# A streaming encoder step on one core: the first closing weight's halves pinned among the last gate projections, and the output weight's last halves moved into the first output pair

## The chip, the cores and the metric

The program runs on one core of a Trainium2 chip. The metric is the device time of one execution in microseconds (us), lower being better. TensorE (PE in the profile) does matrix products and transposes; its weight load is listed apart as PEld. VectorE (DVE), ScalarE (ACT) and GpSimd (POOL) do the elementwise work, and transfers are issued from the queues of SyncE (SP) and POOL.

## The reference

The layer normalises its rows, projects them to `q, k, v`, three gate inputs and a pooling input, runs two token mixers, and merges them:

```python
z = rmsnorm(x, norm_g) @ w_in                  # q k v ga u gb mg, 1024 columns each (mg 2048)
att = stick_breaking(q, k, v)                  # 8 heads x 128, causal
pb = multi_scale_pool(u, ...) * pool_scale     # trailing means, per-group linear map
y_a = (att * silu(ga)) @ w_br_a
y_b = (pb * silu(gb)) @ w_br_b
gate = sigmoid(mg)
m = gate[..., :1024] * y_a + gate[..., 1024:] * y_b
y = rmsnorm(x + m @ w_out, final_g)
```

There are 2048 prompt rows and 64 sample rows (the latter with a cache of 4096 positions), all in float32.

## The kernel before

**Number format.** Every float32 operand is used as two fp32r tiles, `hi` (a copy rounded by ScalarE, line 81) and `lo` (the rest, a subtraction on VectorE, line 82). A product of two operands is three matmuls: hi by hi, hi by lo, lo by hi. Making both tiles of an operand is called its split below; `split` is the helper at lines 76 to 82.

**Stages.** The projections, the attention and the pooling of the two row halves come first and take some three quarters of the program. The last piece of that part, called the gate stretch here, projects 15 column slabs of 128 of the merge gate for the second half of the rows (`merge_gate(1, 1)` to `merge_gate(1, 15)`). A slab has two groups of 512 rows, and a group is 24 matmuls into one of two PSUM buffers `pj` (lines 284 to 286). ScalarE then takes the sigmoid of the group (`sgm`, line 302), which frees the PSUM buffer, and SP stores it to DRAM (line 306). The slab's weights come as two loads of 256 KB (`raw`, line 272, three buffers) and are split into `whi` and `wlo` (two buffers), a slab ahead.

**What runs beside the gate stretch.** `run` interleaves the slabs with the generator `before_closing` (from line 955), in steps set by an estimate of TensorE time. It has 21 steps: four and four for the weight sums of `w_br_a` and `w_br_b`, four for the first row forms, and nine for the first forms of `w_br_a`. The closing multiplies 1024 x 1024 weights as 2 x 2 blocks with seven block products instead of eight, so it needs, beside the blocks `b11, b21, b22`, four differences of blocks `t1` to `t4`. `weight_sums` makes these on POOL: loads (line 904), subtractions (906) and stores to the DRAM tensor `tw_d` (907). `forms` reads blocks and differences back in halves of 512 KB (`wraw`, two buffers, line 934), and splits each half. The call in `before_closing` is for `b11, b21, t1, t2` of `w_br_a`: eight halves, the last four of them read from `tw_d`.

**What sets the order.** In this first part the kernel fixes the order on TensorE only. On the other engines and on SP, a scheduler that works from its own estimates of durations orders the instructions within each engine. From the closing on, the order on TensorE, VectorE, ScalarE and SP is the order of the code; POOL keeps the scheduler's.

**The closing.** For `w_br_a` and then `w_br_b`, three row blocks of 704 rows pass through seven products `p` = 0 to 6, so `order` has 42 entries `s`, each with two column halves `cc`. `emit` multiplies a finished block with its gate and writes it (for `w_br_b`, after adding the first branch, `mp`); it also issues the loads of the gates and of `mp` two and three blocks ahead. The counter h = 2s + cc drives `weights_at(h)`, which runs the next step of `forms`: a table `when` says at which h. A step splits one half and issues the load of the half after next into the buffer that comes free.

**The output pairs.** The last stage multiplies the merged rows by `w_out` in eight pairs of 128 rows, again with seven products of 12 matmuls each, in this order: `x = a11 b11`, `z = a12 b21`, `x += s2 t2`, `y = s1 t1`, `x += s3 t3`, `y += s4 b22`, `x += a22 t4`. Between them ScalarE copies partial sums out (`kept`, line 998), VectorE adds them to the residual rows (`join`, lines 1250 and 1251), and the operands of later products are split: `out_b` makes s1 to s4, `out_c` splits s3 and s4, `out_d` splits a22, `out_a` the next pair's a11 and a12. The merged rows of a pair lie in two tiles `mt` and `mb` with one buffer each, so `fetch(n + 1)` can load `mb` only when the split of a22 has read the old one. The halves of `w_out`'s last blocks, `b22` and `t4`, are split at h = 83, 84, 85 and 87 in the kernel before: the first at the end of the last entry of the closing, the second just ahead of the first pair, the third behind the first `kept` of pair 0, and the fourth behind the third.

Of the kernel before, what the change touches and what calls it, by code (L numbers as in the profile page):

```python
# [8 lines left out]
F32 = mybir.dt.float32  # L9
F32R = mybir.dt.float32r  # L10
AF = mybir.ActivationFunctionType
ALU = mybir.AluOpType
# [3 lines left out]
P = 128  # L16
# [28 lines left out]
def kernel(  # L45
# [6 lines left out]
    nc = tc.nc  # L52
# [92 lines left out]
    with ExitStack() as front:  # L145
# [777 lines left out]
                    nc.gpsimd.dma_start(tw_d[i, j, k * P:(k + 1) * P, :], out)  # L923
            return compute

        def form_half(i, nm, k):

            if nm[0] == "t":
                src = tw_d[i, int(nm[1]) - 1]
            else:  # L930
                r, c = (int(x) - 1 for x in nm[1:])
                src = weights[i][r * 512:(r + 1) * 512, c * 512:(c + 1) * 512]
            raw = wright.tile([P, 2, 512], F32, name="wraw", bufs=2)
            nc.sync.dma_start(raw, src[k * P:(k + 2) * P].rearrange("(k p) c -> p k c", p=P))

            def halves():
                if k == 0:
                    wf[i, nm] = [wpool[nm].tile([P, 4, 512], F32R, name=f"{nm}{part}") for part in ("hi", "lo")]
                hi, lo = wf[i, nm]
                split(hi[:, k:k + 2], lo[:, k:k + 2], raw)  # L940
            return halves

        def forms(i, nms):

            todo = [(nm, k) for nm in nms for k in (0, 2)]
            ahead = [form_half(i, *h) for h in todo[:2]]
            yield 1.0
            for n in range(len(todo)):
                ahead.pop(0)()
                if n + 2 < len(todo):  # L950
                    ahead.append(form_half(i, *todo[n + 2]))
                yield 1.0

        def row_form():
# [4 lines left out]
        def before_closing():  # L959
            yield from weight_sums(0)  # L960
            yield from weight_sums(1)
            for p in range(2):
                hi, lo = rf[p] = row_form()
                for k in (0, 2):
                    raw = wright.tile([P, 2, 512], F32, name="wraw", bufs=2)
                    src = aT_d[p * 512 + k * P:p * 512 + (k + 2) * P, 0:NR].rearrange("(k p) r -> p k r", p=P)
                    nc.sync.dma_start(raw[:, :, 0:NR], src)
                    split(hi[:, k:k + 2], lo[:, k:k + 2], raw[:, :, 0:NR])
                    yield 1.0
            yield from forms(0, ("b11", "b21", "t1", "t2"))  # L970
# [21 lines left out]
    ahead = {}  # L992
# [58 lines left out]
    def out_c(n):  # L1051
        group(n, ("s3", "s4"), s34.pop(n))
# [6 lines left out]
    with tc.manual_schedule(engines={E.PE, E.DVE, E.Activation, E.SP}):  # L1059
# [79 lines left out]
        when = {}  # L1139
        for i, base, nms, at in ((0, 2, WFORMS[4:], [5, 6, 7, 8, 9, 10]),  # L1140
                                 (1, 28, WFORMS, [30 + (8 * h) // 5 for h in range(14)]),
                                 (2, 70, WFORMS, [71 + h for h in range(10)] + [83, 84, 85, 87])):
            when.setdefault(base, []).append((i, nms))
            for h in at:
                when.setdefault(h, []).append(None)
# [21 lines left out]
        for s, (i, t, p) in enumerate(order):  # L1167
            r = rf.pop(s)
            more = s - p + 7 < len(order)
            for cc in range(2):  # L1170
                if p == 0:
                    xs_[cc] = bpsum.tile([P, 2, 512], F32, name="x")
                elif p in (1, 3):
                    ys_[cc] = bpsum.tile([P, 2, 512], F32, name="y")
                acc = (xs_ if p in (0, 2, 4, 6) else ys_)[cc]
                for j in range(2):
                    c = 2 * cc + j
                    product(acc[:, j, 0:NR], wf[i, WFORMS[p]], r, p in (0, 1, 3),
                            slice(c * P, (c + 1) * P), slice(0, NR))
                out = acc[:, :, 0:NR]  # L1180
                if p == 0:
                    x1[cc] = kept(out, "x1")
                elif p == 1:
                    emit(out, x1[cc])
                elif p == 2:
                    x2[cc] = kept(out, "x2")
                elif p == 3:
                    x5[cc] = kept(out, "x5")
                elif p == 4:
                    emit(out, x5[cc])  # L1190
                elif p == 5:
                    emit(out, x2[cc])
                else:
                    emit(out, None)
                if cc == 1:
                    make(s + 2)
                    if p == 0:
                        sum4()
                    if more and p == 5:
                        sum3()  # L1200
                    if more and p == 6:
                        sum12()
                if not more and (p, cc) == (4, 1):
                    rowx.close()
                    pool = ctx.enter_context(tc.tile_pool(name="back", bufs=1, side="left"))
                    fetch(0)
                weights_at(2 * s + cc)
                if more and (p, cc) in ((2, 0), (3, 0), (5, 0), (5, 1)):
                    load_rows(s + 7 - p, {2: "r11", 3: "r21", 5: ("r12", "r22")[cc]}[p])
                if not more and (p, cc) == (6, 0):  # L1210
                    xts = residuals(0)


# [39 lines left out]
        def accumulator(nm):  # L1253
            return bpsum.tile([P, 2, 512], F32, name=nm)[:, 0]

        weights_at(84)
        for n, (_, r) in enumerate(pairs):
            wo = {nm: wf.get((2, nm)) for nm in WFORMS}
            f = {nm: of.pop((n, nm)) for nm in ("a11", "a12", "s2", "s1")}
            last = n + 1 == len(pairs)  # L1260
            x = accumulator("x")
            product(x, f["a11"], wo["b11"], True, cols, whole)
            x1 = kept(x, "x1")
            if n:
                norm_sums(1)
            else:
                weights_at(85)
            z = accumulator("y")
            product(z, f["a12"], wo["b21"], True, cols, whole)
            join(xts[0], left, z, x1)  # L1270
            if n:
                norm_root()
            out_c(n)
            f.update((nm, of.pop((n, nm))) for nm in ("s3", "s4"))
            if not last:
                fetch(n + 1)
            else:
                tail = [pool.tile([P, 4, 256], F32, name=nm) for nm in ("mt", "mb")]
                for h in range(2):
                    src = m_d[h * 512:(h + 1) * 512, 1024:RA].rearrange("(k p) r -> p k r", p=P)  # L1280
                    nc.sync.dma_start(tail[h][:, :, 0:DEC], src)
            product(x, f["s2"], wo["t2"], False, cols, whole)
            x2 = kept(x, "x2")
            if n:
                norm_scale()
            y = accumulator("y")
            product(y, f["s1"], wo["t1"], True, cols, whole)
            x5 = kept(y, "x5")
            if n == 0:
                weights_at(87)  # L1290
                out_d(0)
                wo["t4"] = wf[2, "t4"]
                acc = [pool.tile([P, 2], F32, name=f"acc{i}") for i in range(5)]
                for b in range(2):
                    t = gates.tile([P, 2, NR], F32, name="fg_bc", tag="sg", bufs=5)
                    g_bc.append(t.rearrange("p a b -> p (a b)")[:, 0:512])
                    nc.sync.dma_start(g_bc[b], final_g.rearrange("(a d) -> a d", a=1)[:, b * 512:(b + 1) * 512].broadcast_to([P, 512]))
            if not last:
                out_a(n + 1)
            else:  # L1300
# [75 lines left out]
```

## Time and profile before

| What | Value |
|---|---|
| Time, median of 3 runs | 2799.86 us (2798.79 to 2799.97) |
| Time of the profiled execution | 2798.5 us |
| Its span, first to last instruction | 2796.8 us, so 1.7 us lie around it |
| Mean granted TensorE clock | 0.992 |
| VectorE, ScalarE, POOL busy | 66%, 45%, 21% |
| Matmuls in the trace | 15052 |
| DRAM traffic | 232.46 MB read, 108.65 MB written |

Times in the rows of the profile are microseconds from the start of the span. A timeline row gives start, duration, engine, line, operation, output and inputs, and in brackets how long the engine had been idle before it and what ended that. A row of the wait view gives the engine and line that waited, what released it, total, number of times and the longest. A window row gives, for one stretch, the busy time and the number of instructions of each engine, the granted clock of TensorE, the share of the DMA engines and GB/s. DMA-issuing instructions have short durations of their own; the transfer itself lies behind them.

### The profile page before, as it was taken

Reading aid. Unit: us, or ns where it says so; the run is one execution under the profiler, and the core shown is the slowest. Engines: PE = TensorE matmul, PEld = TensorE weight load, DVE = VectorE, ACT = ScalarE, POOL = GpSimd, SP = SyncE. Lnnn points to the kernel's source line nnn. Section 1 sums busy time; section 2 is a strip of 40 time slices with the busy share of each in tenths; the row PEclk is TensorE's granted clock in tenths of the full one; section 3 lists DMA queues with packets and bytes.
Section 4 is the critical chain, followed back from the end, with each engine's and each line's share of the span. In section 5 each row is a group of like instructions: output and inputs, shape, how many; then the busy total and the mean of one; then the engine's idle time right before and its main releaser. Section 6 shows DMA issues by size and latency. Waiting matters only on the chain.

```text
span 2796.8 us, 41823 instructions
## 1 busy us (share of the span) xinstructions
PE 2706.3 (97%) x15052; PEld 2361.4 (84%) x15052; DVE 1836.2 (66%) x2843; ACT 1267.2 (45%) x2520; POOL 582.0 (21%) x1285
## 2 busy tenths in 40 slices
PE   6999999999999999999999999999997999999898
PEld 5988899989998988888888888887785889999786
DVE  6555555577768684577888788885543127786776
ACT  4445444455555553455555555553222213333343
POOL 2112222220000002223332333231006401100001
PEclk9999999999999999999999999999999999999999
DMA  4224222234454445211111111112337647777653
GB/s 145 78 86 126 72 71 71 77 108 151 147 160 149 151 144 164 65 47 49 57 54 42 54 57 48 44 50 89 106 125 262 197 148 265 263 260 236 219 163 117
DMA packets 344397, 343.87 MB, mean 123 GB/s; under 512 B 30062, under 2 KB 286558, under 8 KB 344188
## 3 DMA queue, kind: packets, MB, share of 16 engines
q1 hardware_dynamic: 329756, 294.26, 33.9%
q0 software_dynamic: 14432, 46.93, 4.7%
q8 instruction: 118, 1.93, 0.3%
q14 instruction: 91, 0.75, 0.1%
HBM read 232.46 MB, written 108.65 MB: 122 GB/s over the span
## 4 chain that ended last, share of the span: by engine, by line
PE 81%; DVE 6%; issue 6%; DMA 4%; POOL 2%; ACT 1%; SPq 0%; POOLq 0%; DVEq 0%; ACTq 0%
PE pj L284 16%; PE pj L286 16%; PE pj L285 16%; PE tr L638 4%; PE att L655 2%; PE att L654 2%; PE att L653 2%; PE z L627 2%; PE z L626 2%; PE z L625 2%; PE x L983 2%; PE x L985 2%; PE x L987 2%; PE y L983 1%; PE y L985 1%
## 5 line engine op out<-in xcount | busy, mean ns | idle before, releaser
L284 PE MATMUL pj<-hhi,whi 128*128 128x512 f32 (+2 forms) x2608 | 947.3, 363 | 19.6 <-ACT sgm L302 19.6
L286 PE MATMUL pj<-hhi,wlo 128*128 128x512 f32 (+2 forms) x2608 | 918.9, 352 | 0.5 <-DVE wlo L82 0.5
L285 PE MATMUL pj<-hlo,whi 128*128 128x512 f32 (+2 forms) x2608 | 917.7, 352 | 0.1
L284 PEld LDWEIGHTS pj<-hhi,whi 128*128 128x128 f32 x2608 | 495.1, 190 | 81.2 <-ACT sgm L302 21.8
L286 PEld LDWEIGHTS pj<-hhi,wlo 128*128 128x128 f32 x2608 | 492.3, 189 | 66.5 <-DVE wlo L82 1.0
L285 PEld LDWEIGHTS pj<-hlo,whi 128*128 128x128 f32 x2608 | 494.1, 189 | 59.0 <-DVE hlo L82 0.4
L579 DVE TENSOR_TENSOR_SCAN om<-om 128x513 f32<-128x513 f32 (+3 forms) x356 | 387.4, 1088 | 212.3 <-POOL om L561 108.4
L569 ACT ACTIVATE om<-z 128x512 f32<-128x512 f32 (+2 forms) x320 | 171.4, 535 | 322.3 <-PE z L627 271.9
L82 DVE TENSOR_TENSOR wlo<-raw,whi 128x512 fp32r<-128x512 f32 x248 | 180.5, 733 | 198.3 <-ACT whi L81 197.5
L581 POOL COPY carry<-om 128x1 f32<-128x1 f32 x356 | 77.9, 219 | 918.8 <-DVE om L579 878.3
L582 DVE TENSOR_TENSOR be<-be,om 128x512 f32<-128x512 f32 (+3 forms) x356 | 230.1, 646 | 31.4
L81 ACT CAST whi<-raw 128x512 fp32r<-128x512 f32 x256 | 158.2, 623 | 174.8 <-PE pj L285 157.8
L81 ACT CAST a<-tr 128x512 fp32r<-128x512 f32 (+2 forms) x356 | 188.0, 528 | 100.4 <-PE tr L638 89.9
L82 DVE TENSOR_TENSOR a<-tr,a 128x512 fp32r<-128x512 f32 (+2 forms) x356 | 215.2, 605 | 23.8 <-ACT a L81 21.7
L638 PE MATMUL tr<-ident,be 128*128 128x128 f32 x1088 | 175.7, 274 | 6.1 <-DVE be L582 3.6
L638 PEld LDWEIGHTS tr<-ident,be 128*128 128x128 f32 x1088 | 136.2, 140 | 44.7 <-DVE be L582 8.4
L570 ACT ACTIVATE be<-z 128x512 f32<-128x512 f32 (+2 forms) x320 | 170.0, 531 | 0.0
L653 PE MATMUL att<-a,v 128*128 128x512 f32 (+1 forms) x320 | 133.2, 416 | 0.0
L561 POOL TENSOR_SCALAR_AFFINE_SELECT om<-om 128x128 f32<-128x128 f32 x128 | 50.7, 396 | 354.3 <-ACT om L569 354.2
L574 POOL COPY om<-carry 128x1 f32<-128x1 f32 x224 | 123.8, 553 | 2.7 <-DVE be L582 0.7
L655 PE MATMUL att<-a,v 128*128 128x512 f32 (+1 forms) x320 | 118.5, 370 | 3.6 <-DVE a L82 3.3
L654 PE MATMUL att<-a,v 128*128 128x512 f32 (+1 forms) x320 | 117.3, 367 | 0.0
(312 smaller groups left out, 4676.6 us busy)
## 6 DMA issues: line engine op xcount, KB each, us to landing
raw<-in_w_in_dram SPq DMA_DIRECT2D x256, 256.0 KB, 3.2
sg<-sm_d SPq DMA_DIRECT2D x48, 352.0 KB, 6.3
kraw<-in_cache_k_dram SPq DMA_DIRECT2D x64, 256.0 KB, 3.5
vraw<-in_cache_v_dram SPq DMA_DIRECT2D x64, 256.0 KB, 2.9
sm_d<-sgm SPq DMA_DIRECT2D x48, 256.0 KB, 2.2
wraw<-tw_d SPq DMA_DIRECT2D x24, 512.0 KB, 4.7
out_dram<-nat SPq DMA_DIRECT2D x42, 256.0 KB, 2.3
r<-aT_d SPq DMA_DIRECT2D x12, 704.0 KB, 7.3
```

Of the source, the lines that this page charges most:

```text
L81: nc.scalar.copy(hi, src)
L82: (nc.gpsimd if eng == "g" else nc.vector).tensor_tensor(lo, src, hi.bitcast(F32), op=ALU.subtract)
L284: nc.tensor.matmul(ps[:, 0:n], whi[:, k], hhi[:, k, c0:c0 + n], start=k == 0, stop=False)
L285: nc.tensor.matmul(ps[:, 0:n], whi[:, k], hlo[:, k, c0:c0 + n], start=False, stop=False)
L286: nc.tensor.matmul(ps[:, 0:n], wlo[:, k], hhi[:, k, c0:c0 + n], start=False, stop=k == KT - 1)
L569: nc.scalar.activation(om[:, off:512], z[:, off:512], AF.Sigmoid, scale=-SCALE)
L579: nc.vector.tensor_tensor_scan(rev, rev, rev, 1.0, op0=ALU.mult, op1=ALU.bypass)
L582: nc.vector.tensor_tensor(be[:, off:512], be[:, off:512], om[:, off + 1:513], op=ALU.mult)
L638: nc.tensor.transpose(tr[:, i * P:(i + 1) * P], be[:, off + j * P:off + (j + 1) * P], ident)
L653: nc.tensor.matmul(self.acc[:, s], vhi[:, js], ahi[:, s], start=first, stop=False)
L654: nc.tensor.matmul(self.acc[:, s], vlo[:, js], ahi[:, s], start=False, stop=False)
L655: nc.tensor.matmul(self.acc[:, s], vhi[:, js], alo[:, s], start=False, stop=last)
```

## The change

**Pinned halves.** A new helper `pinned` calls `tc.keep_in_program_order`, which ties an instruction behind the one that was recorded before it on the same engine. `form_half` and `forms` get an argument `pin`; where it is true, the load, the ScalarE copy and the VectorE subtraction of a half are pinned. Only the call in `before_closing` passes it. `form_half` writes the two operations of the split out, at lines 945 and 946 of the changed file; they are the same operations for every half.

**Later halves of the output weight.** The last four steps of `w_out`'s forms move from h = 83, 84, 85, 87 to 85, 86, 87, 88. The call `weights_at(84)` ahead of the pairs goes; within pair 0, 85 stays behind the first `kept`, 86 stands ahead of `out_c`, 87 behind the second `kept`, and 88 where 87 stood. Because `b22` is now made within the pair, its product takes it from `wf` and not from the dictionary filled at the pair's start.

**Residual rows.** The loads of pair 0's residual rows are written one column half and one product earlier, at (p, cc) = (5, 1) of the last row block instead of (6, 0).

```diff
+        def pinned(ins, pin):
+            if pin:
+                tc.keep_in_program_order(ins)
...
-        def form_half(i, nm, k):
+        def form_half(i, nm, k, pin=False):
...
-            nc.sync.dma_start(raw, src[k * P:(k + 2) * P].rearrange("(k p) c -> p k c", p=P))
+            pinned(nc.sync.dma_start(raw, src[k * P:(k + 2) * P].rearrange("(k p) c -> p k c", p=P)), pin)
...
-                hi, lo = wf[i, nm]
-                split(hi[:, k:k + 2], lo[:, k:k + 2], raw)
+                hi, lo = (t[:, k:k + 2] for t in wf[i, nm])
+                pinned(nc.scalar.copy(hi, raw), pin)
+                pinned(nc.vector.tensor_tensor(lo, raw, hi.bitcast(F32), op=ALU.subtract), pin)
...
-            yield from forms(0, ("b11", "b21", "t1", "t2"))
+            yield from forms(0, ("b11", "b21", "t1", "t2"), True)
...
-                                 (2, 70, WFORMS, [71 + h for h in range(10)] + [83, 84, 85, 87])):
+                                 (2, 70, WFORMS, [71 + h for h in range(10)] + [85, 86, 87, 88])):
...
-                if not more and (p, cc) == (6, 0):
+                if not more and (p, cc) == (5, 1):
                     xts = residuals(0)
...
-        weights_at(84)
...
             if n:
                 norm_root()
+            else:
+                weights_at(86)
             out_c(n)
...
             if n:
                 norm_scale()
+            else:
+                weights_at(87)
...
-                weights_at(87)
+                weights_at(88)
                 out_d(0)
...
-            product(y, f["s4"], wo["b22"], False, cols, whole)
+            product(y, f["s4"], wf[2, "b22"], False, cols, whole)
```

Three places show what this does to the order of instructions. The first is ScalarE in the gate stretch, after the last row form (`rhi`); `b11hi`, `b21hi`, `t1hi` and `t2hi` are the copies of the pinned halves, `sgm` the sigmoid that frees a group's PSUM buffer, `whi` the copy of a slab's weights. Before:

```order
L81 CAST b21hi<-wraw 128x1024
L81 CAST t1hi<-wraw 128x1024
L302 ACTIVATE sgm<-pj 128x512
L81 CAST whi<-raw 128x512
L302 ACTIVATE sgm<-pj 128x512
L81 CAST whi<-raw 128x512
L81 CAST t1hi<-wraw 128x1024
L302 ACTIVATE sgm<-pj 128x512
L81 CAST t2hi<-wraw 128x1024 x2
L302 ACTIVATE sgm<-pj 128x512
L81 CAST whi<-raw 128x512 x2
```

After, at the end of the stretch, with the last three sigmoids in one row:

```order
L945 CAST t1hi<-wraw 128x1024
L81 CAST whi<-raw 128x512
L302 ACTIVATE sgm<-pj 128x512
L81 CAST whi<-raw 128x512
L945 CAST t2hi<-wraw 128x1024
L302 ACTIVATE sgm<-pj 128x512
L945 CAST t2hi<-wraw 128x1024
L302 ACTIVATE sgm<-pj 128x512 x3
```

Of the 31 sigmoids from the last group of the slab before the stretch on, the eight copies stood between the third and the ninth, with two of them in one gap at three places; now the first stands behind the 18th and the last behind the 28th, with at most one between two sigmoids.

The second place is SP's queue at the first of these halves. Before, behind the last load of a row form (`wraw<-aT_d`):

```order
L967 DMA wraw<-aT_d 128x2x352
L934 DMA wraw<-in_w_br_a_dram 128x2x512
L306 DMA sm_d<-sgm 128x512
L272 DMA raw<-in_w_in_dram 128x4x128 x2
L934 DMA wraw<-in_w_br_a_dram 128x2x512 x2
L306 DMA sm_d<-sgm 128x512
L934 DMA wraw<-in_w_br_a_dram 128x2x512
L934 DMA wraw<-tw_d 128x2x512
L306 DMA sm_d<-sgm 128x512
```

After, the first of these loads stands behind 16 more stores of sigmoids; the first of the rows below is the store of the 18th:

```order
L306 DMA sm_d<-sgm 128x512
L939 DMA wraw<-in_w_br_a_dram 128x2x512 x2
L306 DMA sm_d<-sgm 128x512
L939 DMA wraw<-in_w_br_a_dram 128x2x512
L272 DMA raw<-in_w_in_dram 128x4x128 x2
L306 DMA sm_d<-sgm 128x512 x2
L272 DMA raw<-in_w_in_dram 128x4x128
L939 DMA wraw<-in_w_br_a_dram 128x2x512
L272 DMA raw<-in_w_in_dram 128x4x128
L306 DMA sm_d<-sgm 128x512
L939 DMA wraw<-tw_d 128x2x512
```

The loads of the pinned halves moved behind those stores, and loads of slab weights (`raw`) now stand behind some of them.

The third place is ScalarE at the first output pair: `s_27190` and `s_27189` are s2 and s1, `s_27191` and `s_27192` s3 and s4, the copies from `x` and `y` are the partial sums. Before:

```order
L81 CAST rhi<-s_27190 128x512
L81 CAST rhi<-s_27189 128x512
L81 CAST b22hi<-wraw 128x1024 x2
L998 COPY x_27226<-x 128x512
L81 CAST t4hi<-wraw 128x1024
L81 CAST rhi<-s_27191 128x512
L81 CAST rhi<-s_27192 128x512
L998 COPY x_27269<-x 128x512
L998 COPY x_27284<-y 128x512
L81 CAST t4hi<-wraw 128x1024
```

After:

```order
L81 CAST rhi<-s_27190 128x512
L81 CAST rhi<-s_27189 128x512
L1004 COPY x_27216<-x 128x512
L945 CAST b22hi<-wraw 128x1024 x2
L81 CAST rhi<-s_27191 128x512
L81 CAST rhi<-s_27192 128x512
L1004 COPY x_27265<-x 128x512
L945 CAST t4hi<-wraw 128x1024
L1004 COPY x_27284<-y 128x512
L945 CAST t4hi<-wraw 128x1024
```

The first partial sum moved ahead of both copies of `b22`. On VectorE in the same place the two subtractions for `b22` stood together; now the two joins of `z` and the first partial sum stand between them, and both subtractions for `t4` come behind the split of s3 and s4. On SP nothing moved there: the loads of `t4`, the residual rows and the next pair's merged rows stand in the order of before. On TensorE and POOL the order is the same throughout.

More of the change, by code (lines that the diff above doesn't have):

```diff
@@ L938, in halves, with forms @@
                     wf[i, nm] = [wpool[nm].tile([P, 4, 512], F32R, name=f"{nm}{part}") for part in ("hi", "lo")]
-                hi, lo = wf[i, nm]
-                split(hi[:, k:k + 2], lo[:, k:k + 2], raw)
+                hi, lo = (t[:, k:k + 2] for t in wf[i, nm])
+                pinned(nc.scalar.copy(hi, raw), pin)
+                pinned(nc.vector.tensor_tensor(lo, raw, hi.bitcast(F32), op=ALU.subtract), pin)
             return halves
-        def forms(i, nms):
+        def forms(i, nms, pin=False):
             todo = [(nm, k) for nm in nms for k in (0, 2)]
-            ahead = [form_half(i, *h) for h in todo[:2]]
+            ahead = [form_half(i, *h, pin) for h in todo[:2]]
             yield 1.0
@@ L950, in forms @@
                 if n + 2 < len(todo):
-                    ahead.append(form_half(i, *todo[n + 2]))
+                    ahead.append(form_half(i, *todo[n + 2], pin))
                 yield 1.0
```

## The prediction, made before the changed kernel ran

> **What bounds the kernel now.** I read the page first, then windows, then the waits of TensorE stretch by stretch, then the timeline around its longest gaps.
>
> ```profile
> span 2796.8 us, 41823 instructions
> PE 2706.3 (97%) x15052; PEld 2361.4 (84%) x15052; DVE 1836.2 (66%) x2843; ACT 1267.2 (45%) x2520; POOL 582.0 (21%) x1285
> ```
>
> TensorE is busy for 97% of the span, so the kernel is bound by its matmuls, and only its gaps and its slow clock can be had back by a new order. The windows show where these are in the gate stretch (about 2090 to 2282 us).
>
> ```profile
> 2100.00:2150.00 50.00, 36.56 (x148) 28.27 (x146) 19.12 (x14) 13.13 (x19) 32.67 (x41) 0.95 0.74 246
> 2150.00:2200.00 50.00, 43.85 (x179) 34.98 (x180) 13.59 (x11) 12.32 (x20) 32.60 (x42) 0.92 0.81 272
> 2200.00:2250.00 50.00, 50.00 (x216) 40.21 (x215) 8.94 (x10) 10.51 (x19) 7.97 (x9) 1.00 0.40 130
> ```
>
> The third window is the stretch as it runs undisturbed: 216 matmuls in 50 us, 0.2315 us each. The first two hold 148 + 179 = 327 where 432 would fit, with a lower granted clock. The waits of TensorE there (2089 to 2300 us) have this row at the top:
>
> ```profile
> PE pj L284 <- ACT sgm L302: 19.6, 5, 10.3
> ```
>
> So TensorE waited 19.6 us, in five pieces, for sigmoids that free its PSUM buffers. The timeline of ScalarE, TensorE, SP and POOL around the longest piece shows why the sigmoid was late:
>
> ```profile
> 2152.88 1.05 ACT L81 CAST t1hi<-wraw 128x1024 fp32r<-128x1024 f32 x1 [20.09 <-DMA wraw<-tw_d]
> 2153.84 0.59 ACT L302 ACTIVATE sgm<-pj 128x512 f32<-128x512 f32 x1
> 2154.48 0.79 PE L284 MATMUL pj<-hhi,whi 128*128 128x512 f32 x1 [10.33 <-ACT sgm L302]
> 2147.99 0.37 SPq L934 DMA_DIRECT2D wraw<-tw_d  x1
> 2145.63 0.56 POOL L907 DMA_DIRECT2D tw_d<-ws  x1 [0.30 <-POOL ws L906]
> 2149.93 0.56 POOL L907 DMA_DIRECT2D tw_d<-ws  x1 [0.30 <-POOL ws L906]
> ```
>
> ScalarE stood 20.09 us at the copy of `t1`'s second half. Its load went out at 2147.99, when POOL's store of the last quarter of `t1`, issued at 2145.63, had landed. The sigmoid that TensorE needed was queued behind the copy. The scheduler had set the halves ahead of the sums they read.
>
> The second place is output pair 0; the waits from 2600 to 2645 us:
>
> ```profile
> PE x L983 <- ACT x L998: 6.4, 1, 6.4
> PE x L983 <- DVE xo L1251: 3.7, 1, 3.7
> PE x L987 <- DVE rlo L82: 0.7, 1, 0.7
> ```
>
> **The gate stretch, part by part.** *Removed:* the early copies and loads. The two windows lack 432 - 327 = 105 matmuls, and 105 x 0.2315 = 24.3 us. Of that 19.6 us are waits, all five within these windows, and 4.7 us the slow restart. As a bound on the restart, the clocks 0.95 and 0.92 over 50 us each give 2.5 + 4.0 = 6.5 us, which makes 26.1 us in all; but the clock is also low while TensorE stands still, and that time is in the 19.6 already. I take the count, 24.3 us, with 19.6 and 26.1 as bounds.
>
> The Trainium skill, page "TensorE: Matmul & The Clock Gate", section "HAM oscillation — how this bites in real kernels", prices a restart at the throttled time times one half. By that the throttled time of 13.0 us in the two windows would cost 6.5 us, and the sum would be 26.1 us; the trace's count of matmuls speaks for less.
>
> *Added:* the same 24 instructions (eight halves of three) later, so no new work. Each pinned half is a load, a copy and a subtraction, and what is queued behind them can now be late. The rows for the size of this:
>
> ```profile
> wraw<-in_w_br_a_dram SPq DMA_DIRECT2D x6, 512.0 KB, 5.1
> wraw<-tw_d SPq DMA_DIRECT2D x24, 512.0 KB, 4.7
> raw<-in_w_in_dram SPq DMA_DIRECT2D x256, 256.0 KB, 3.2
> 2153.96 1.23 DVE L82 TENSOR_TENSOR t1lo<-wraw,t1hi 128x1024 fp32r<-128x1024 f32 x1 [17.97 <-ACT t1hi L81]
> 2276.11 0.60 ACT L302 ACTIVATE sgm<-pj 128x512 f32<-128x512 f32 x1 [5.00 <-PE pj L286]
> 2281.72 0.60 ACT L302 ACTIVATE sgm<-pj 128x512 f32<-128x512 f32 x1 [5.01 <-PE pj L286]
> 2131.30 0.34 SPq L306 DMA_DIRECT2D sm_d<-sgm  x1
> ```
>
> A group takes 5.6 us (2281.72 - 2276.11). The tightest place is the first half: its copy stands between sigmoids 18 and 19, its load behind the store of sigmoid 18. Counted from the end of group 18: sigmoid 0.6, issue of the store 0.34 and of the load 0.37 make 1.3; the load lands at 1.3 + 5.1 = 6.4; the copy of 1.05 ends at 7.5, sigmoid 19 at 8.1. It was due to begin at 5.6, but TensorE needs its buffer only for group 21, at 11.2. So 3.1 us of cover are left, and this wait costs nothing unless that load takes over 8.2 us. Every later copy stands at least one whole group behind its load. On SP the third load waits for the first half's subtraction, 7.5 + 1.23 = 8.7 us; behind it stand two slab weights, which land by about 8.7 + 0.4 + 0.4 + 3.2 = 12.7 us, while the copy that takes the first of them stands behind sigmoid 21, at 16.8. POOL stored the last quarter of `t2` at 2149.93, and the fifth half, the first from `tw_d`, is now behind the store of sigmoid 22, near 2282 - 24 - 9 x 5.6 = 2208. POOL has nothing left to do for it by then. The last copy, behind sigmoid 28, is three groups ahead of the closing. So I cost the additions at nothing. What is late next is nothing in this stretch: TensorE at 5.6 us a group.
>
> **The output pair, part by part.** The rows, by engine:
>
> ```profile
> 2614.73 1.14 ACT L81 CAST rhi<-s 128x512 fp32r<-128x512 f32 x2 [11.19 <-DVE s L1046]
> 2615.77 1.99 ACT L81 CAST b22hi<-wraw 128x1024 fp32r<-128x1024 f32 x2
> 2617.66 0.57 ACT L998 COPY x<-x 128x512 f32<-128x512 f32 x1
> 2622.79 1.05 ACT L81 CAST t4hi<-wraw 128x1024 fp32r<-128x1024 f32 x1 [4.56 <-DMA wraw<-tw_d]
> 2626.08 0.58 ACT L998 COPY x<-y 128x512 f32<-128x512 f32 x1 [0.71 <-PE y L987]
> 2626.56 1.05 ACT L81 CAST t4hi<-wraw 128x1024 fp32r<-128x1024 f32 x1
> 2617.79 2.35 DVE L82 TENSOR_TENSOR b22lo<-wraw,b22hi 128x1024 fp32r<-128x1024 f32 x2
> 2625.02 0.69 DVE L1250 TENSOR_TENSOR xo<-xo,x 128x512 f32<-128x512 f32 x1
> 2626.42 1.28 DVE L82 TENSOR_TENSOR rlo<-s,rhi 128x512 fp32r<-128x512 f32 x2
> 2628.79 0.68 DVE L82 TENSOR_TENSOR a<-mb,a 128x512 fp32r<-128x512 f32 x1
> 2619.03 1.51 SPq L934 DMA_DIRECT2D wraw<-tw_d  x2
> 2629.50 0.36 SPq L1010 DMA_DIRECT2D mb<-m_d  x1
> 2633.96 0.69 DVE L82 TENSOR_TENSOR rlo<-mb,rhi 128x512 fp32r<-128x512 f32 x1 [3.88 <-ACT rhi L81]
> 2618.29 0.79 PE L983 MATMUL x<-t2hi,rhi 128*128 128x512 f32 x1 [6.41 <-ACT x L998]
> 2636.19 0.76 PE L983 MATMUL x<-t4hi,a 128*128 128x512 f32 x1 [3.73 <-DVE xo L1251]
> ```
>
> *First gap.* The first partial sum stood behind both copies of `b22`. It now starts where they did, 2617.66 - 2615.77 = 1.9 us earlier, and so does `x += s2 t2`. The gap of 6.4 shrinks to 4.5 us. The 0.7 us at `t3` goes too, since the split of s3 then ends ahead of the `y` product.
>
> *Last gap.* It is the end of a chain: second half of `t4`, split of a22, load of `mb` into its one buffer, split of the next a12, the joins, `x += a22 t4`. The chain sets the end, not the first gap. Its head, the copy at 2626.56, waited behind the copy from `y` (2626.08). That one is 1.9 us earlier now, which would let the head start at 2624.7. But its load is later: between the subtractions of `b22` stand the two joins, 2626.42 - 2625.02 = 1.4 us, so the second ends at 2617.79 + 2.35 + 1.4 = 2621.5, and the load takes as long as the first one did, 2622.79 - 2619.03 = 3.8. The head starts at 2625.3, 1.3 us earlier than before, and the rest of the chain keeps its lengths. So `x += a22 t4` starts at 2634.9 instead of 2636.2, after a gap of about 3.7 + 1.9 + 0.7 - 1.3 = 5.0 us. That is 1.3 us from 2.6 that the two earlier gaps gave. Bounds: 1.9 if the load is no hindrance; and a loss of 1.2 if it takes 6.3, as loads of this size for the same weight do here (head at 2627.8):
>
> ```profile
> wraw<-in_w_out_dram SPq DMA_DIRECT2D x14, 512.0 KB, 6.3
> ```
>
> I take 1.3, from the row for the same tensor at the same moment. By the section "What's actually happening" of the same page of the Trainium skill, an idle window of about 3.4 us halves the clock; both gaps stay above that, so no restart would be saved here, and the sum has none. The earlier residual rows cost and bring nothing: their loads keep their place on SP.
>
> **The sum.** 24.3 + 1.3 = 25.6 us. The profiled execution took 2798.5 (its span and 1.7 us around it), so 2772.9 by it; that execution lies 1.36 us under the median of the runs, 2799.86, against which the forecast is 2774.3 us.
>
> **The rivals.** *Partly pinned down (10%).* The pinned copies catch ScalarE while POOL's second set of sums still fills the DMA engines (share 0.81 in the second window). A load that takes 10.6 us (`mp`, issued at 2601.82 and used at 2612.42, below) would pass the 8.2 us above by 2.4, and one to three such halves give 2.4 to 7 us back: 2776.7 to 2781. For it: those sums run until after 2200. Against it: `b11`'s loads stood in the same traffic and took 5.1.
>
> ```profile
> 2601.82 0.51 SPq L1118 DMA_DIRECT2D mp<-mp_d  x1
> 2612.42 0.89 DVE L1133 TENSOR_TENSOR sg<-sg,mp 128x704 f32<-128x704 f32 x1 [2.54 <-DMA mp<-mp_d]
> ```
>
> *The output pair loses (6%).* The second `t4` load is the slow one: 24.3 - 1.2 = 23.1, 2776.8 us.
>
> *The pins don't matter (2%).* If the copies meet POOL's sums as before, nothing moves: 2799.9. The new order and a margin of some 50 us speak against it.
>
> *Slower (2%).* SP becomes the bound of the gate stretch. Eight halves have 13 groups, 73 us, from sigmoid 18 on. If every load waited out its predecessor's whole chain (landing, copy 1.05, subtraction 1.23), the stretch would be longer than TensorE's from a landing of 73 / 8 - 2.3 = 6.8 us on, as slab weights stand behind the loads. At 10.6 us that is 8 x 3.8 = 30 us against 25.6 won: 2804. Against it: two buffers let two loads overlap, and 5.1 is under 6.8.
>
> **How the numbers follow.** The forecast has 80%; its own range is 2772 to 2777, from the bounds of the pair and some 2 us on the count. With half of the first rival the range is 2771.5 to 2778.5. A measurement of this kernel tells about 0.2%, 5.6 us, from no change. Forecast, first and second rival all lie over 5.6 us under 2799.86, 96%; I keep 94% for faster, 3% for no difference and 3% for slower, for what the rivals don't name.
>
> **What would show it.** Right: the windows of the gate stretch have 216 matmuls per 50 us throughout, TensorE's wait for `sgm` at line 302 is under 1 us, and SP's loads from `tw_d` wait for subtractions and not for POOL's stores; in pair 0 the wait for the first partial sum is near 4.5 us and the one ahead of `t4` near 5. Wrong: waits for `sgm` between sigmoids 18 and 28 (first rival), a wait of TensorE for `wlo` or `whi` there (the slower one), or the copy of `t4`'s second half over 11.8 us behind that of s2 (2626.56 - 2614.73 before; 10.6 by the forecast), which would be the second rival.

## The result and the profile after

The changed kernel takes 2775.52 us (median of four runs, 2774.83 to 2776.29); the kernel before took 2799.91 us on the same chip (2798.79 to 2801.09). The ratio is 0.9913, with a 95% interval of 0.9896 to 0.993, and the gain 24.4 us, where 25.6 was forecast. The page of the changed kernel begins so:

```profile
span 2774.0 us, 41821 instructions
PE 2706.2 (98%) x15052; PEld 2364.5 (85%) x15052; DVE 1835.5 (66%) x2843; ACT 1268.3 (46%) x2520; POOL 582.6 (21%) x1285
```

TensorE does the same matmuls in a span 22.8 us shorter. That its busy time is the same over the whole span is a coincidence. Between the first and the last sigmoid of the gate stretch it fell from 172.0 to 167.6 us, because fewer matmuls ran at the slow clock, while it rose by 4.3 us ahead of the stretch and in the closing of this execution. The windows of the gate stretch show where the waits went (the engines stand in the order TensorE, its weight load, VectorE, ScalarE, POOL):

```profile
2100.00:2150.00 50.00, 50.00 (x216) 40.21 (x215) 15.01 (x13) 12.77 (x22) 33.21 (x42) 1.00 0.78 250
2150.00:2200.00 50.00, 50.00 (x216) 40.23 (x215) 10.37 (x10) 10.44 (x18) 31.75 (x41) 1.00 0.80 253
2200.00:2250.00 50.00, 50.00 (x216) 40.23 (x215) 17.45 (x15) 16.18 (x24) 8.05 (x9) 1.00 0.56 183
```

All three windows have 216 matmuls and the full clock. POOL and the DMA engines are as busy in the first two as they were, so the sums still run there; only the copies that need them now come later. The waits of TensorE from 2080 to 2290 us have no row for `sgm`, and these two are all:

```profile
PE x L991 <- DVE rlo L82: 1.2, 1, 1.2
PE x L989 <- issue: 0.8, 1, 0.8
```

The timeline around the first pinned half, from sigmoid 18 to sigmoid 20, with the first load from `tw_d` and the copy that takes it:

```profile
2186.37 0.60 ACT L302 ACTIVATE sgm<-pj 128x512 f32<-128x512 f32 x1 [4.26 <-issue]
2187.38 0.98 SPq L939 DMA_DIRECT2D wraw<-in_w_br_a_dram  x2
2192.72 1.05 ACT L945 CAST b11hi<-wraw 128x1024 fp32r<-128x1024 f32 x1 [5.75 <-DMA wraw<-in_w_br_a_dram]
2193.67 0.59 ACT L302 ACTIVATE sgm<-pj 128x512 f32<-128x512 f32 x1
2197.57 0.60 ACT L302 ACTIVATE sgm<-pj 128x512 f32<-128x512 f32 x1 [2.28 <-issue]
2212.00 0.37 SPq L939 DMA_DIRECT2D wraw<-tw_d  x1
2216.57 1.05 ACT L945 CAST t1hi<-wraw 128x1024 fp32r<-128x1024 f32 x1 [0.86 <-DMA wraw<-tw_d]
```

ScalarE does wait 5.75 us here, and sigmoid 19 starts 7.3 us after sigmoid 18 instead of 5.6. That is 1.7 us late, TensorE has the other PSUM buffer, and by sigmoid 20 (2197.57, 11.2 us after sigmoid 18) the delay is gone. The load from `tw_d` goes out at 2212.00. SP's waits from 2180 to 2260 us name subtractions on VectorE ahead of the loads of halves and no store of POOL.

The second place, output pair 0: first TensorE's waits from 2580 to 2625 us, then the timeline.

```profile
PE x L989 <- DVE xo L1257: 6.0, 1, 6.0
PE x L989 <- ACT x L1004: 3.3, 1, 3.3
```

```profile
2591.99 1.14 ACT L81 CAST rhi<-s 128x512 fp32r<-128x512 f32 x2 [9.82 <-DVE s L1052]
2593.04 0.58 ACT L1004 COPY x<-x 128x512 f32<-128x512 f32 x1
2593.51 2.00 ACT L945 CAST b22hi<-wraw 128x1024 fp32r<-128x1024 f32 x2
2602.60 1.05 ACT L945 CAST t4hi<-wraw 128x1024 fp32r<-128x1024 f32 x1 [1.05 <-DMA wraw<-tw_d]
2605.54 0.36 SPq L1016 DMA_DIRECT2D mb<-m_d  x1
2609.41 0.62 ACT L81 CAST rhi<-mb 128x512 fp32r<-128x512 f32 x1 [4.72 <-DMA mb<-m_d]
2593.67 0.79 PE L989 MATMUL x<-t2hi,rhi 128*128 128x512 f32 x1 [3.27 <-ACT x L1004]
2612.30 0.77 PE L989 MATMUL x<-t4hi,a 128*128 128x512 f32 x1 [5.98 <-DVE xo L1257]
```

The first partial sum now stands ahead of the copies of `b22`, and TensorE's first gap is 3.27 us instead of 6.41. The last gap grew from 3.73 to 5.98 us: it still ends with the chain through `t4`'s second half and the load into the single buffer of `mb`.

To see where the span went, both traces are cut at the same instructions, which are the first and the last sigmoid of the gate stretch, the first matmul of pair 0 and that of pair 1. The two traces have these points at 2090.02, 2281.72, 2606.18, 2640.62 before and at 2091.46, 2259.17, 2584.71, 2617.45 after. So the gate stretch went from 191.70 to 167.71 us (-24.0) and pair 0 from 34.44 to 32.74 (-1.7); everything ahead of the stretch took 1.4 us more, the closing 1.1 more and the rest 0.4 more. The sum is -22.8, the difference of the spans.

### The profile page after: what moved, and what is told of

Same layout as the page of the kernel before. It is cut to its first block, busy times and chain, and to the rows that moved or that the text cites. A ratio compares the mean times of both kernels' runs of the same rounds, so it can differ in the third digit from the quotient of the medians.

```text
span 2774.0 us, 41821 instructions
## 1 busy us (share of the span) xinstructions
PE 2706.2 (98%) x15052; PEld 2364.5 (85%) x15052; DVE 1835.5 (66%) x2843; ACT 1268.3 (46%) x2520; POOL 582.6 (21%) x1285
## 4 chain that ended last, share of the span: by engine, by line
PE 84%; issue 6%; DVE 5%; DMA 2%; ACT 1%; POOL 1%; SPq 0%; POOLq 0%; DVEq 0%; ACTq 0%
PE pj L284 17%; PE pj L285 17%; PE pj L286 17%; PE tr L638 4%; PE att L655 2%; PE att L654 2%; PE z L627 2%; PE att L653 2%; PE z L626 2%; PE z L625 2%; PE x L989 2%; PE x L991 2%; PE x L993 2%; PE y L989 1%; PE y L993 1%
```

## The experiments

The theory: the two parts of the change add up; nearly all the gain is the gate stretch, where ScalarE stood at copies of halves whose sums POOL had not yet stored, and the pair gives a little over 1 us because its last gap hangs on a chain that ends at the `mb` buffer. The rivals: one part loses and the other covers it; or the early place of the halves is bad in itself, whether their sums are ready or not.

**Each part alone.** From the changed kernel, first the pair's part undone, of which these are some of the lines (the pins remain):

```diff
-            (2, 70, WFORMS, [71 + h for h in range(10)] + [85, 86, 87, 88])):
+            (2, 70, WFORMS, [71 + h for h in range(10)] + [83, 84, 85, 87])):
...
+        weights_at(84)
...
-                weights_at(88)
+                weights_at(87)
```

> The kernel before with the pins alone; the output pair is as before. Theory: the whole gain comes from the gate stretch, so the time is 24 us under the kernel before, 2775.5 to 2776.5 us, with no wait of TensorE for a sigmoid in the gate stretch, and the waits of output pair 0 as before (6.4, 0.7 and 3.7 us). Rival: the pair's part carries several of the 24.4 us measured; then this kernel is over 2778 us.

Then the pins undone (the pair's part remains):

```diff
-            yield from forms(0, ("b11", "b21", "t1", "t2"), True)
+            yield from forms(0, ("b11", "b21", "t1", "t2"))
```

> The kernel before with the output pair's part alone, no pins. The prediction's term of 1.3 us would give 2798.6 us. What the two traces say by now: the chain into the last product of the pair is some 1.2 us earlier, but the clock after its longer gap stays low for longer, so little or nothing is left: 2798.8 to 2800 us. The gate stretch keeps its 19.6 us of waits either way.

Pins alone: 2776.88 us (2776.11 to 2777.91), ratio 0.992 [0.9907, 0.9933] against the kernel before on that chip (2800.17 us), 0.4 us above the range expected. The pair's part alone: 2798.26 us (2795.39 to 2802.93), ratio 0.9996 [0.9988, 1.0005], 0.5 us below its range. In the first there is no wait for `sgm` and the stretch takes 167.71 us; its pair keeps the old gaps. The waits of its pair 0, and then those of the pair's part alone (the gate stretch first, then the pair):

```profile
PE x L989 <- ACT x L1004: 5.9, 1, 5.9
PE x L989 <- DVE xo L1257: 3.9, 1, 3.9
```

```profile
PE pj L284 <- ACT sgm L302: 17.5, 5, 11.9
PE x L989 <- DVE xo L1257: 5.8, 1, 5.8
PE x L989 <- ACT x L1004: 4.2, 1, 4.2
```

So the pins carry the gain, 23.3 us by the medians. The pair's part is too small for a median to show, but not for the traces: pair 0 takes 34.44, 34.00, 34.79, 33.79 and 34.50 us in five kernels of this study with the old pair (mean 34.3) and 32.74, 33.63 and 32.70 in three executions with the new one (mean 33.0). That is 1.3 us between the means; the nearest two values of the groups lie 0.2 us apart.

**The halves early, but with their sums ready.** The kernel before, with `t1` and `t2` of the first closing weight read from a block of the weight itself in place of POOL's sums. The bytes are the same, and no load waits for POOL; the output is then that of another weight. The last argument of `forms` is here `ready` and not the pin. The order is still the scheduler's, and it is not quite that of before: on ScalarE the second half of `t1` and both halves of `t2` stand one or two sigmoids earlier.

```diff
-            if nm[0] == "t":
+            if nm[0] == "t" and ready:
+                src = weights[i][512:1024, 512:1024]
+            elif nm[0] == "t":
                 src = tw_d[i, int(nm[1]) - 1]
...
-            yield from forms(0, ("b11", "b21", "t1", "t2"))
+            yield from forms(0, ("b11", "b21", "t1", "t2"), True)
```

> The kernel before, its early order kept, but the halves of t1 and t2 of the first closing weight are read from a block of the weight and not from the sums that GpSimd stores (the first branch is multiplied by wrong differences; no work is left out). Theory: ScalarE's wait for those stores is what made the sigmoids late. Then the three gaps of TensorE that fall on t1 and t2 (3.8, 10.3 and 1.7 us, and the slow clock after them) go, and the two on b11 and b21 (1.7 and 2.1 us) stay: about 20 us less, 2779 to 2782 us. Rival: the early place itself is the trouble, since copies crowd between sigmoids and their loads share the DMA engines with GpSimd's; then most of the waits stay and the time is over 2792 us.

It took 2788.48 us (2785.55 to 2792.7), ratio 0.9961 [0.9949, 0.9973]: 11.7 us under the kernel before and 11.6 above the pins alone. Its wait for `sgm`, its first window and the copy that ends its longest wait:

```profile
PE pj L284 <- ACT sgm L302: 9.4, 4, 4.8
```

```profile
2100.00:2150.00 50.00, 40.58 (x161) 31.32 (x160) 22.40 (x17) 17.44 (x25) 31.07 (x39) 0.93 0.90 301
```

```profile
2133.46 1.04 ACT L81 CAST t1hi<-wraw 128x1024 fp32r<-128x1024 f32 x1 [4.42 <-DMA wraw<-in_w_br_a_dram]
```

Neither theory holds as stated. The first falls by half: with nothing to wait for on POOL, 9.4 of the 19.6 us stay, and the window still lacks 216 - 161 = 55 matmuls, 12.7 us at 0.2315. ScalarE waits for plain loads now, at a DMA share of 0.90. Two theories of that half were left. Either the place is bad by itself (eight halves among six groups, with two buffers), or it is bad because POOL's sums, with their own loads and stores, keep the DMA engines busy there.

**Early and ready, with the sums left out.** The same kernel without POOL's weight sums; `t` halves of both closing weights are now read from a block of the weight. The sums' loads, subtractions and stores all stand in POOL's queue, and in the traces the order on SP and ScalarE around the early halves is that of the last kernel. Work is left out, so only the gate stretch is to be read: the closing took 2.7 us more than in the kernel before, and what lies behind pair 0 took 2.4 us less.

```diff
-            if nm[0] == "t" and ready:
+            if nm[0] == "t" and i < 2:
...
-            yield from weight_sums(0)
-            yield from weight_sums(1)
+            for _ in range(8):
+                yield 1.0
```

> The kernel with both closing weights' t halves ready in DRAM and placed early as in the former order (the earlier run of that kind: 9.4 us of waits for sgm over 2100 to 2290, a gate stretch of 180.5 us, DMA engines 0.90 busy), and now POOL's weight sums left out with their loads and stores, so that the DMA engines are quieter; this leaves out work, and only the gate stretch is to be read. Theory, shared DMA engines: loads land in some 3.5 us, the waits for sgm fall to 2 to 4 us and the stretch to 170 to 174 us. Rival, the early place alone: the waits stay at 8 us or more and the stretch at 178 us or more.

The time was 2776.37 us (2773.81 to 2777.71), and the gate stretch 167.71 us with no wait for `sgm` at all: better than the 170 to 174 us expected of quieter DMA engines. The DMA view from 2095 to 2160 us, of the kernel with the sums and then of the one without (queue totals, and the loads of the halves with their median time to landing):

```profile
DMA packets 12339, 19.26 MB, mean 296 GB/s; under 512 B 1024, under 2 KB 6913, under 8 KB 12335
wraw<-in_w_br_a_dram SPq DMA_DIRECT2D x8, 512.0 KB, 6.0
```

```profile
DMA packets 10816, 11.31 MB, mean 174 GB/s; under 512 B 545, under 2 KB 7356, under 8 KB 10812
wraw<-in_w_br_a_dram SPq DMA_DIRECT2D x8, 512.0 KB, 4.2
```

```profile
2100.00:2150.00 50.00, 50.00 (x216) 40.24 (x215) 18.78 (x21) 20.04 (x29) 0.00 (x0) 1.00 0.58 182
```

With 4.2 us in place of 6.0 for a load, the same early order costs TensorE nothing: the eight copies go through in 23.7 us (2107.07 to 2130.73) instead of 34.4 (2114.50 to 2148.86), and a group is 5.6 us. So the place alone does no harm; POOL's sums make it harmful.

The sums' work holds up a half in two places, which the two traces show apart. Without the sums each of the eight subtractions on VectorE takes 1.22 or 1.23 us; with them three of the eight take 2.2 to 2.6 us, and POOL subtracts at the same moment. The second half of `t1`, with the sums and then without:

```profile
2138.62 2.55 DVE L82 TENSOR_TENSOR t1lo<-wraw,t1hi 128x1024 fp32r<-128x1024 f32 x1 [1.85 <-ACT t1hi L81]
2124.93 1.23 DVE L82 TENSOR_TENSOR t1lo<-wraw,t1hi 128x1024 fp32r<-128x1024 f32 x1 [2.46 <-ACT t1hi L81]
```

The four second halves pass through one `wraw` buffer, so each load waits for the subtraction ahead of it. From the first of these loads to the last of these copies it is 35.9 us with the sums (2111.96 to 2147.81) and 24.1 without (2105.58 to 2129.68). Of the 11.8 us between them, the four loads make 10.4 and that one subtraction 1.3. So nearly all of it is slow loads.

The stalls before thus had one source, POOL's sums, and two ways in: the last halves waited for the sums to be stored (191.70 - 180.54 = 11.2 us of the stretch), and the others were held up by the sums' work, in the main by slow loads (180.54 - 167.71 = 12.8 us). The split is rough, because the kernel with the ready halves has some copies earlier than the kernel before. The trace of before says much the same by itself. Of the loads of the eight halves only two waited for a store of the sums, one of them 16.3 us (SP's waits from 2100 to 2165 us):

```profile
SPq L934 <- DMA tw_d<-ws: 17.3, 2, 16.3
```

TensorE's first three waits for `sgm` (1.71, 2.08 and 3.80, together 7.6 us) end before the load that waited 16.3 us goes out, at 2147.99; the other two (10.33 and 1.67, together 12.0 us) end after it.

**Only one queue pinned.** Pins alone, with the pin kept on the loads and taken off the copies and subtractions:

```diff
-                pinned(nc.scalar.copy(hi, raw), pin)
-                pinned(nc.vector.tensor_tensor(lo, raw, hi.bitcast(F32), op=ALU.subtract), pin)
+                nc.scalar.copy(hi, raw)
+                nc.vector.tensor_tensor(lo, raw, hi.bitcast(F32), op=ALU.subtract)
```

> The pins alone, and of them only the loads' queue: ScalarE's copies and POOL's subtractions of the first closing weight are left to the scheduler. Theory, that one pinned queue is enough since the scheduler may set a copy no earlier than the load that feeds it: the order on ScalarE comes out the same, no wait for sgm, the gate stretch (first to last sigmoid of that part) 167.7 us, 2776 to 2778 us. Rival, that each queue needs its pin: a copy slips ahead of a gate's group again and a wait of over 5 us for sgm comes back, 2782 us or more.

It took 2776.87 us (2774.18 to 2782.87), ratio 0.9922 [0.9907, 0.9937], as the pins alone did. (The subtractions of a split run on VectorE, not on POOL as the expectation has it.) The gate stretch took 167.72 us and had no wait for `sgm`. The order on ScalarE did not come out the same: the first copy stands where it did, the others up to three sigmoids earlier. A pinned load is still enough here, since the scheduler sets what uses it behind it.

**The chain behind the last gap.** The changed kernel with a second buffer for `mb`, so that the next pair's load does not wait for the split of a22 (and the same for the tail rows behind the last pair):

```diff
-        merged[n] = [pool.tile([P, 4, 256], F32, name=nm) for nm in ("mt", "mb")]
+        merged[n] = [pool.tile([P, 4, 256], F32, name=nm, bufs=nb) for nm, nb in (("mt", 1), ("mb", 2))]
```

> The changed kernel with two buffers for the tile of the lower merged rows, so that the next pair's load need not wait for the split of a22. Theory: this load's wait sets the last gap of pair 0 (6.0 us), so the load goes out with its neighbour some 6 us earlier, the gap falls to about 2 us and the slow clock behind it goes: 4 to 6.5 us less, 2769 to 2771.5 us. Rival: the splits of t4 or the joins bind just behind it; then the gap stays over 4 us and the time is 2774 to 2775.5 us.

It took 2768.08 us (2767.19 to 2770.3), ratio 0.9889 [0.9874, 0.9904]: 7.4 us under the changed kernel by the medians, more than the theory's 4 to 6.5. Pair 0 takes 27.25 us instead of 32.74, so 5.5 us lie there (5.8 against the mean of the three traces with the new pair); ahead of pair 0 this trace is 3.0 us shorter, in parts that the buffer does not touch, and behind it the two agree. Its last gap:

```profile
PE x L989 <- DVE xo L1257: 2.1, 1, 2.1
```

Two windows each, from 2580 to 2620 us, of the changed kernel and then of this one:

```profile
2580.00:2600.00 20.00, 16.43 (x73) 13.68 (x72) 15.72 (x21) 6.44 (x11) 2.15 (x3) 0.91 0.72 265
2600.00:2620.00 20.00, 14.02 (x52) 11.03 (x52) 11.92 (x18) 7.26 (x13) 0.00 (x0) 0.83 0.55 170
```

```profile
2580.00:2600.00 20.00, 15.99 (x65) 12.75 (x64) 14.04 (x19) 6.78 (x10) 2.02 (x3) 0.91 0.70 248
2600.00:2620.00 20.00, 17.90 (x79) 14.53 (x78) 15.70 (x30) 10.89 (x21) 0.12 (x1) 1.00 0.53 177
```

The window that holds the last gap has 79 matmuls instead of 52, at the full clock instead of 0.83. Because of these 3.0 us the windows do not hold quite the same work, so the length of the pair is the better measure. The gap is 3.9 us shorter, and at 2.1 us no slow clock follows it. That the single `mb` buffer set 3.9 of the 6.0 us is shown; the 2.1 us that remain were not taken apart.

**The first gap as well.** On top of the second buffer, the sum and splits behind pair 0's s2 issued ahead of the last gate's last step:

```diff
                 else:
+                    if not more and cc == 1:
+                        make(s + 2)
                     emit(out, None)
                 if cc == 1:
-                    make(s + 2)
+                    if more or p < 6:
+                        make(s + 2)
```

> The changed kernel with two buffers of mb, and the sum and load behind pair 0's s2 issued ahead of the last gate's last step. Theory, that s2 only stands behind that gate's sg and mp transfers in the queues: the first gap (3.3 us in the changed kernel) and the half-speed matmuls behind it go, 3 to 6 us less than with two buffers alone, 2762 to 2765 us, and no wait of over 1 us for an x copy at the start of pair 0. Rival, that t4's halves and b22's copies are next in line at once: the gap moves by a few us and keeps its length, 2767 to 2769 us.

It took 2767.32 us (2766.07 to 2769.19), ratio 0.9885 [0.9871, 0.99]; the two-buffer kernel was timed on another chip, and the difference of 0.8 us between them is within their runs. The rival's numbers came, though not quite by its mechanism. TensorE's waits from 2560 to 2660 us, and the second half of `t4` on ScalarE with its load:

```profile
PE x L989 <- DVE xo L1260: 3.7, 1, 3.7
PE x L989 <- DVE sg L1137: 0.4, 1, 0.4
```

```profile
2591.11 2.91 SPq L939 DMA_DIRECT2D wraw<-tw_d  x2
2597.42 1.05 ACT L945 CAST t4hi<-wraw 128x1024 fp32r<-128x1024 f32 x1 [0.71 <-DMA wraw<-tw_d]
2603.47 0.76 PE L989 MATMUL x<-t4hi,a 128*128 128x512 f32 x1 [3.67 <-DVE xo L1260]
```

The wait for the x copy is gone, and pair 0 takes 24.95 us instead of 27.25. But `t4` hangs on the subtractions of `b22`, which free its buffers, and the last gap grew from 2.1 to 3.7 us, long enough for the first matmul behind it to take 0.76 us. Of the 3.8 us of the first gap in the two-buffer kernel, 2.3 are won in pair 0, and its first matmul came 1.15 us later in this execution.

**The changed kernel again**, on the chip of the last experiments:

> The changed kernel once more, beside the others of this set. Both theories expect 2775 to 2777 us and, if the slower first 90 us of the closing matmuls (0.1611 us from start to start, against 0.1589 in the kernel before) belongs to one execution and not to the kernel, a spacing that can be another one this time, between 0.1585 and 0.1615.

2775.01 us (2773.84 to 2779.08), ratio 0.9915 [0.99, 0.993]; span 2772.1 us, gate stretch 167.71 us, pair 0 33.63 us. The closing, from the last sigmoid to pair 0, took 324.1 us against 324.5 before and 325.5 in the first trace of the same kernel. Windows from 2290 to 2330 us, first trace, then this one:

```profile
2290.00:2330.00 40.00, 40.00 (x250) 40.00 (x249) 31.92 (x29) 13.15 (x13) 6.49 (x10) 1.00 0.81 274
```

```profile
2290.00:2330.00 40.00, 40.00 (x253) 40.00 (x253) 32.28 (x30) 14.45 (x13) 6.78 (x11) 1.00 0.81 276
```

So 1.1 us of the closing in the first trace belonged to that execution and not to the change.

## Why the prediction was right, point by point

**The gate stretch: right in size.** The count of missing matmuls gave 24.3 us; the stretch gave 24.0, and every window came out at 216 matmuls. By the rule of the Trainium skill, page "TensorE: Matmul & The Clock Gate", section "HAM oscillation — how this bites in real kernels", that the loss is half of the throttled time, it would have been 26.1 by estimate, 2.1 us more than the trace shows. The granted clock of a window is also low while TensorE stands still (0.50 from 2150 to 2154.4 us in the kernel before, with no matmul in that time), and the count of matmuls takes such time once only.

**The cause: too narrow.** "The scheduler had set the halves ahead of the sums they read" is true, and by the experiments it explains some 11 of the 24.0 us. The other 13 or so were halves held up by the sums' work, in the main by slow loads, which the prediction took for harmless ("`b11`'s loads stood in the same traffic and took 5.1"). That the number held in spite of this is luck in part. Counting missing matmuls needs no cause, and the new place has the sums stored and enough cover for slow loads. It is not clear of POOL's work, whose last subtraction ends at 2210.9 us: the first pinned load took 5.3 us there. By the split above, a forecast for a kernel that only made the sums earlier would have been some 13 us wrong; no such kernel was run.

**The additions at nothing: right, and near.** Of the first pinned half the forecast said that its copy ends 7.5 us after group 18 and the limit is 11.2; sigmoid 19 started 7.3 us behind sigmoid 18, and TensorE did not wait. Not every later copy stood a whole group behind its load, as the prediction had it: the first copy from `tw_d` came 4.6 us behind, and ScalarE waited 0.86 us for it. But no later copy made TensorE wait either, so the first rival (partly pinned down) did not come, nor the slower one: there is no wait for `whi` or `wlo`.

**The pair: right in sum and in its chain, off in the gaps.** The chain's head, the copy of `t4`'s second half, came 10.6 us behind the copy of s2 in all three traces with the new pair, as forecast, against 11.5 to 12.4 in the five with the old one. Pair 0 became shorter by about as much, 1.3 us by the means, which is the forecast value (1.7 in the first trace). The gaps were forecast as 4.5 and 5.0 us. The first came as 3.27, 4.07 and 4.21 in the three traces, the last as 5.98, 5.82 and 5.83; with the old pair they were 5.20 to 6.41 and 3.73 to 4.31. By the means the first shrank by 2.0 us, where 1.9 was forecast, and the last grew by 1.9 instead of 1.3. The first also depends on when s2 arrives: its copy stands 7.3 to 8.55 us behind pair 0's first matmul in these eight traces, with either order. The forecast counted no gain at the slow clock; pair 0 without its waits took 23.3 us instead of 23.9 by the means, in single traces 22.7 to 24.1. That the chain sets the end of pair 0, and not the first gap, is what the second `mb` buffer showed.

**The sum.** Forecast 25.6 us, measured 24.4 by the medians. In the first trace the terms make 24.0 + 1.7 = 25.7, and 2.9 us are given back in parts that the change does not touch: 1.4 ahead of the stretch, 1.1 in the closing, 0.4 behind. The first two did not come back when the same kernel ran again (-0.2 and -0.3 us against before). They are a difference between executions. The part behind pair 0 took 0.7 us more than before the second time as well. It goes with the pins: 156.5 to 156.9 us in the six traces with pinned loads, 156.15 to 156.18 in the three without them that have POOL's sums. Why is left open.

## What to carry to other kernels

Where an in-order engine holds both the instruction that frees a PSUM buffer and a copy that waits for a load, place that copy by when its load can land at the traffic of that moment, not by when its data exist: here about half the stall was missing data and the other half mostly slow loads, and pinning the load alone cured both. Price such a stall by the matmuls that are missing in its windows, since that holds whatever the cause turns out to be. A gap at the end of a chain does not shrink with an earlier gap: look for what the chain waits for (here a single buffer, worth 5.5 to 6 us of pair 0, against 1.3 for the reordering around it).

## What the runs showed of the hardware

In 40 us in which TensorE never waited, at a granted clock of 1.00, the pace of the same 128x352 matmuls differed between executions of one kernel: 250 against 253 in the two windows above. The whole closing up to pair 0 took 325.5 and 324.1 us in these two. The kernel without the sums, whose closing reads other numbers, took 327.2 us for it (2259.34 to 2586.51). No run here tells what sets that pace.

The length of a gap alone did not decide whether slow matmuls followed it. Behind 3.27 us the first matmul took 0.79 us (the row above). Behind the 2.1 us of the two-buffer kernel, and behind a gap of 2.52 us in the gate stretch of the kernel with the ready halves, there was no slow clock:

```profile
2606.14 0.47 PE L989 MATMUL x<-t4hi,a 128*128 128x512 f32 x1 [2.10 <-DVE xo L1257]
```

But in the trace of the pair's part alone two gaps of 1.88 and 2.49 us in the gate stretch were followed by a few matmuls at the full pace and then by some 3 us of matmuls 0.43 us apart, against 0.23. The first matmul behind the 2.49 us and the fifth:

```profile
2122.55 0.50 PE L284 MATMUL pj<-hhi,whi 128*128 128x512 f32 x1 [2.49 <-ACT sgm L302]
2123.92 0.63 PE L285 MATMUL pj<-hlo,whi 128*128 128x512 f32 x1
```

Behind the 4.07 us of the second trace of the changed kernel, too, the first matmuls ran at the full pace and the next at 0.43. The Trainium skill, page "TensorE: Matmul & The Clock Gate", section "What's actually happening", puts the idle window at about 3.4 us; here gaps of 1.88, 2.49 and 3.27 us were already enough in single cases.
